# Last MLP in two phases, its first matrix as seven block products

## The chip, the cores and the metric

The kernel runs on one core of a Trainium2 chip. The core has five engines with a queue of instructions each: TensorE (PE, with its weight loads PEld shown apart), VectorE (DVE), ScalarE (ACT), GpSimd (POOL) and SyncE (SP), which issues nearly all DMAs here. The metric is device time in microseconds (us), the median of several runs.

## The reference

Two decoder layers on a sequence of 1024 tokens with 1024 features, all in float32. Each layer is a mixer (mLSTM in layer 0, latent attention in layer 1) and an MLP; the change is in the MLP of layer 1.

```python
def sqrelu_mlp(h, w1, w2):
    return jnp.square(jax.nn.relu(h @ w1)) @ w2
...
        h = modulate(rmsnorm(x, norm_g[l, 2]), sh2, sc2)
        y = sqrelu_mlp(h, mlp_w1[l], mlp_w2[l])
        x = x + g2[:, None, :] * rmsnorm(y, norm_g[l, 3])
```

`w1` is 1024 x 4096 and `w2` is 4096 x 1024.

## The kernel before

Tokens are worked on in two halves of 512. Activations lie with features on the partitions (eight blocks `k` of 128 features by 512 tokens); a tile `k4` or `hd` holds two such blocks. Every product is made of three passes (`mm3`, L230 to L233): each operand is split into a rounded high part (`hi`, type float32r) and a rest (`lo`), and the three matmuls `lo*hi`, `hi*lo`, `hi*hi` are summed in PSUM. ACT makes the high part by a cast (L189 for weights in `wsplit`, L470 in `split_mod`), DVE the rest by a subtraction (L190, L471).

Buffers are pools by tag: `k4` 24, `hd` 8, `ws` (split weights) 8, `raw` (loaded weights) 4, `tmc` 6, all in SBUF; in PSUM `ps` 2 and `pc` 2 of one bank, `pm` 2 of two banks. A tile that is asked for when all buffers of its tag are taken waits until one is released.

`mlp` (L941) yields steps. A *hidden* step makes one block of 128 hidden features by 512 tokens: one weight load of 512 KB and its split, 24 matmuls of 512 columns, relu, square and split. An *up* step takes finished hidden blocks times rows of `w2` into `y`. For the last half, groups of four are used: four hidden steps of a group are traced in turn with four up steps of the group before, and weights are loaded two steps ahead (`AHEAD`). With `rows=True` the result has tokens on the partitions.

A planner orders the instructions of each engine by a time model, by program order as priority; `tc.high_priority(PRIO)` moves instructions ahead by 300. PE's order is held by `go` (L1806): each step of a stream is issued behind the one before. `two_streams` (L1823) runs the other half's mixer between the steps of an MLP. Before the last MLP stands

```python
    two_streams(mlp(1, hfs[0], u0, [2] * 16, True), mixer1(hfs[1], z1, attention_second))
```

that is the first half's last MLP, with the second half's attention, output matrix, residual and norm (`post` L1751, `normed` L476) in it. Then comes the second half's MLP alone, with `all_out` as filler: at each step end one `next` of it. `x_to_rows` (L1564) loads each feature block of the residual stream, turns it by four PE transposes, copies it by ACT and stores it by token rows (`xr`); `rows_out` (L1593) reads those rows, forms the norm of a 128-token row block of the MLP's result (`u0` or `u1`), adds, and stores the output. The order is: turn of the first half, norm of the first half, turn of the second half, and behind the last matmul the norm of the second half.

Of the kernel before, what the change touches and what calls it, by code (L numbers as in the profile page):

```python
# [9 lines left out]
F32 = mybir.dt.float32  # L10
F32R = mybir.dt.float32r
# [3 lines left out]
ALU = mybir.AluOpType  # L15
# [67 lines left out]
def kernel(  # L83
# [54 lines left out]
    def tmc(dt=F32):  # L138
        return sb.tile([P, 512], dt, tag="tmc", bufs=TMC, name=f"tmc_{next(uid)}")
# [13 lines left out]
    def pm():  # L153
        return pp.tile([P, 2, 512], F32, tag="pm", bufs=2, name=f"pm_{next(uid)}")
# [72 lines left out]

    pe_last = [None]

    def mm3(o, lh, ll, rh, rl, start, stop):  # L230
        nc.tensor.matmul(o, ll, rh, start=start, stop=False)  # L231
        nc.tensor.matmul(o, lh, rl, start=False, stop=False)  # L232
        pe_last[0] = nc.tensor.matmul(o, lh, rh, start=False, stop=stop)  # L233


    nc.scalar.preload_act_table_set("natural_log_exp_and_others")
# [239 lines left out]
    def normed(h, xs_, rstd, A, sh):  # L476

        for k in range(KD):
            with paced():
                nc.vector.scalar_tensor_tensor(  # L480
                    xs_[k], xs_[k], A[:, k : k + 1], rstd, ALU.mult, ALU.mult
                )
                split_mod(h.hi[k], h.lo[k], xs_[k], sh[:, k : k + 1])
            if k % 4 == 3:
                yield 1

    def along_tokens(dst, y):
# [450 lines left out]
    NF = DFF // P  # L938
    AHEAD = 2

    def mlp(l, hf, y, sizes, rows=False):  # L941


        w1, w2, h = mlp_w1[l], mlp_w2[l], hf.h2
        hids = {}

        def hidden(f):
            def hid(w):
# [24 lines left out]
        def up_rows(fs, i, last):  # L973
# [40 lines left out]
            def out(ws):  # L1014
                for t in range(t0, t1):
                    if t % 2 == 0:
                        if t > t0:
                            yield "within"
                        b2 = pm()
                    block(b2[:, t % 2], ws, t)  # L1020
# [6 lines left out]
        def up_cols(fs, i, last):  # L1027
            G = len(fs)
            n = KD // G

            def out(w):
                for m in range(i * n, (i + 1) * n):
                    if m % 2 == 0:
                        if m > i * n:
                            yield "within"
                        b2 = pm()
                    pt = b2[:, m % 2]
# [8 lines left out]
        up = up_rows if rows else up_cols  # L1046
        steps, prev, f0 = [], [], 0
        for G in sizes:
            fs = list(range(f0, f0 + G))
# [8 lines left out]
        ready = []  # L1058
        for n in range(len(steps) + AHEAD):
            if n < len(steps):  # L1060
                ready.append(steps[n][0]())
            if n >= AHEAD:
                yield from steps[n - AHEAD][1](ready.pop(0))

                yield steps[(n - AHEAD + 1) % len(steps)][1].__name__


    rope_d = scratch([2, P, S], "rope_d")
# [494 lines left out]

    def x_to_rows(half):  # L1564

        for k in range(KD):
            a, b = tmc(), tmc()
            nc.sync.dma_start(a, xs_blk(k, half))
            yield
            pt = pc()  # L1570
            for t in range(4):
                nc.tensor.transpose(pt[:, ts(t, P)], a[:, ts(t, P)], ident)
            nc.scalar.copy(b, pt)
# [174 lines left out]
    A1 = gain(2, NG(0, 2), adac(0, SC2))  # L1748
    B1 = gate(3, NG(0, 3), adac(0, G2))

    def post(hf, y, B, src, A, sh):  # L1751
# [5 lines left out]
        yield 0  # L1757
        hf.h2 = Split()
        yield from normed(hf.h2, y, rstd, A, sh)

# [126 lines left out]
    rope_perm()  # L1887


    z1 = FH(claim=True)  # L1890
    ya = [None, None]

    def mixer1(hf, z, attention):
# [12 lines left out]
        for _ in wout(b_w_out[0], hf.o, lambda m, pt: evac(y[m], pt)):  # L1906
            yield 0
        yield 1
        yield from post(hf, y, B2, x_cols, A3, adac(1, SH2))
# [6 lines left out]
    u1 = FH(claim=True)  # L1916
# [46 lines left out]
```

## Time and profile before

| what | value |
|---|---|
| runs | 2396.41, 2397.75, 2398.75 us (median 2397.75) |
| profiled execution, first to last instruction | 2395.7 us |
| last MLP of the second half, first to last matmul | 2027.4 to 2387.2 us of the span |
| mean granted clock of PE | 0.997 |

The profiled execution has no time of its own beside its span; the three runs lie 0.7 to 3.1 us above the span. "Busy" is the time in which an engine works on at least one instruction; PE's matmuls overlap, so the distance between the starts of two is what one costs in a row. In a row of the groups view stand line, engine, operation, output<-inputs, shapes, count, then busy us and mean ns of one, then the engine's idle time just before and what ended it.

### The profile page before, as it was taken

The page shows a single profiled execution, that of the slowest core. Times are in us where ns is not written, and L with a number is a line of the kernel's source. Part 1 is how long each engine was busy: PE and PEld are TensorE (multiplying, and loading weights), DVE is VectorE, ACT ScalarE, POOL GpSimd, SP SyncE. Part 2 cuts the span into 40 slices and gives each one's busy share as a digit, 9 for nine tenths or more (in the row PEclk, how much of TensorE's full clock was granted, in tenths as well). Part 3 has the DMA queues.
Part 4 walks back from the last instruction along what each step waited for, and adds up shares of the span by engine and source line. Part 5 has one row for each costly group of instructions (what it writes and reads, how often), then busy time and mean ns, then how long its engine had stood idle before and what let it go on. Part 6 is the DMA issues. An engine that isn't in the chain of part 4 may idle for free.

```text
span 2395.7 us, 30518 instructions
## 1 busy us (share of the span) xinstructions
PE 2364.8 (99%) x11621; PEld 1945.5 (81%) x11621; DVE 1550.3 (65%) x2431; ACT 1054.9 (44%) x1712; POOL 18.3 (1%) x91
## 2 busy tenths in 40 slices
PE   7999999999999999999999999999999999999998
PEld 5888888788888887888888877888888888888886
DVE  6667866858656677877764867766566386353345
ACT  4355334655333454444444554344444353443333
POOL 1000000000000000000000000000000000000000
PEclk9999999999999999999999999999999999999999
DMA  8442654544654745545543444864424354354431
GB/s 310 148 143 81 192 178 134 165 132 150 189 171 152 243 138 179 159 160 186 168 137 114 153 162 153 260 240 133 139 97 150 105 167 128 101 189 140 144 99 62
DMA packets 377106, 374.48 MB, mean 156 GB/s; under 512 B 24355, under 2 KB 282464, under 8 KB 376960
## 3 DMA queue, kind: packets, MB, share of 16 engines
q1 hardware_dynamic: 376672, 372.44, 48.9%
q8 instruction: 91, 1.49, 0.3%
q14 instruction: 55, 0.45, 0.1%
q0 software_dynamic: 288, 0.10, 0.0%
HBM read 313.24 MB, written 59.24 MB: 155 GB/s over the span
## 4 chain that ended last, share of the span: by engine, by line
PE 91%; DVE 4%; DMA 3%; ACT 1%; issue 1%; SPq 0%; DVEq 0%; ACTq 0%
PE ps L231 17%; PE ps L232 17%; PE ps L233 17%; PE pm L231 10%; PE pm L232 10%; PE pm L233 10%; PE pc L1445 1%; PE pc L231 1%; PE pc L233 1%; PE pc L232 1%; PE pm L815 1%; PE pm L1331 1%; DMA raw<-in_mlp_w_dram 1%; DVE wl L190 1%; PE pm L1325 1%
## 5 line engine op out<-in xcount | busy, mean ns | idle before, releaser
L190 DVE TENSOR_TENSOR wl<-raw,wh 128x1024 fp32r<-128x1024 f32 (+2 forms) x366 | 438.7, 1202 | 449.5 <-ACT wh L189 442.3
L189 ACT CAST wh<-raw 128x1024 fp32r<-128x1024 f32 (+2 forms) x366 | 376.0, 1032 | 717.0 <-PE ps L231 392.2
L231 PE MATMUL ps<-k,wl 128*128 128x512 f32 x1528 | 611.0, 400 | 2.3 <-ACT k L671 1.4
L233 PE MATMUL ps<-k,wh 128*128 128x512 f32 x1528 | 601.0, 393 | 0.0
L232 PE MATMUL ps<-k,wh 128*128 128x512 f32 x1528 | 600.9, 393 | 0.0
L231 PEld LDWEIGHTS ps<-k,wl 128*128 128x128 f32 x1528 | 287.0, 188 | 69.7 <-issue 2.9
L233 PEld LDWEIGHTS ps<-k,wh 128*128 128x128 f32 x1528 | 287.0, 188 | 67.3 <-issue 0.5
L232 PEld LDWEIGHTS ps<-k,wh 128*128 128x128 f32 x1528 | 287.5, 188 | 63.6 <-issue 1.7
L198 DVE TENSOR_TENSOR k<-k,pm 128x512 f32<-128x512 f32 (+1 forms) x254 | 210.9, 859 | 107.0 <-PE pm L233 106.5
L231 PE MATMUL pm<-hd,wl 128*128 128x512 f32 x512 | 202.0, 394 | 0.4 <-ACT hd L470 0.4
L233 PE MATMUL pm<-hd,wh 128*128 128x512 f32 x512 | 199.8, 391 | 0.0
L232 PE MATMUL pm<-hd,wh 128*128 128x512 f32 x512 | 199.5, 390 | 0.2 <-DVE hd L471 0.2
L231 PE MATMUL pm<-wh,hd 128*128 128x512 f32 x488 | 192.9, 395 | 3.2 <-ACT raw L1337 2.9
L232 PE MATMUL pm<-wl,hd 128*128 128x512 f32 x488 | 191.3, 392 | 0.0
L233 PE MATMUL pm<-wh,hd 128*128 128x512 f32 x488 | 190.3, 390 | 0.0
L360 DVE SCALAR_TENSOR_TENSOR tma<-raw,cond,tma 128x512 f32<-128x512 f32 x168 | 125.6, 747 | 20.6 <-DMA raw<-in_kv_ada_w_dram 14.6
L471 DVE TENSOR_TENSOR hd<-tmp,hd 128x512 fp32r<-128x512 f32 x128 | 88.3, 690 | 56.8 <-ACT hd L470 56.5
L1337 ACT ACTIVATE raw<-pm,sm 128x128 f32<-128x128 f32 (+3 forms) x64 | 47.5, 742 | 151.3 <-DVE sm L1336 122.7
L232 PEld LDWEIGHTS pm<-hd,wh 128*128 128x128 f32 x512 | 96.2, 188 | 21.3 <-DVE hd L471 0.5
L231 PEld LDWEIGHTS pm<-hd,wl 128*128 128x128 f32 x512 | 96.1, 188 | 21.2 <-ACT hd L470 0.8
L233 PEld LDWEIGHTS pm<-hd,wh 128*128 128x128 f32 x512 | 96.1, 188 | 21.1
L231 PEld LDWEIGHTS pm<-wh,hd 128*128 128x128 f32 x488 | 91.6, 188 | 24.9 <-ACT raw L1337 5.5
(347 smaller groups left out, 3414.5 us busy)
## 6 DMA issues: line engine op xcount, KB each, us to landing
raw<-in_mlp_w_dram SPq DMA_DIRECT2D x256, 512.0 KB, 4.1
raw<-in_ada_w_dram SPq DMA_DIRECT2D x80, 512.0 KB, 4.3
raw<-in_a_w_in_dram SPq DMA_DIRECT2D x48, 512.0 KB, 4.1
xs<-k SPq DMA_DIRECT2D x40, 256.0 KB, 4.8
raw<-in_kv_ada_w_dram SPq DMA_DIRECT2D x16, 512.0 KB, 3.8
raw<-in_a_w_out_dram SPq DMA_DIRECT2D x16, 512.0 KB, 4.6
kd<-k SPq DMA_DIRECT2D x32, 256.0 KB, 3.7
vd<-k SPq DMA_DIRECT2D x32, 256.0 KB, 5.0
```

The costliest lines, as they stand in the source:

```text
L189: nc.scalar.copy(hi[:, :n], r[:, :n])
L190: i = nc.vector.tensor_sub(lo[:, :n], r[:, :n], hi[:, :n].bitcast(F32))
L198: return f(*a, **k)
L231: nc.tensor.matmul(o, ll, rh, start=start, stop=False)
L232: nc.tensor.matmul(o, lh, rl, start=False, stop=False)
L233: pe_last[0] = nc.tensor.matmul(o, lh, rh, start=False, stop=stop)
L360: nc.vector.scalar_tensor_tensor(acc, r[:, kk], cond[:, k : k + 1], acc, ALU.mult, ALU.add)
L471: nc.vector.tensor_sub(lo, u, hi.bitcast(F32))
L815: nc.tensor.matmul(nv[:, r, i], hf.PT[p_][:, r, cs], v[:, 2 * p_ + r], start=g == 0, stop=True,)
L1325: nc.tensor.matmul(o[:, :w], ql, kh, start=True, stop=False)
L1331: nc.tensor.matmul(o[:, :w], qh, kh, start=False, stop=True)
L1337: nc.scalar.activation(pr[:, :n], f, AF.Exp, bias=m, scale=SCALE, accum_out=l)
```

## The change

The second half's last MLP no longer alternates between its two matrices. It has two phases.

Phase one (`seven`) makes all 32 hidden blocks. For each pair of blocks, the product of `w1` (features in two halves, the two blocks) with the tokens' activations (features in two halves, tokens in two halves of 256) is seen as a 2 x 2 by 2 x 2 block product and made of seven block products (the form with few sums by Strassen and Winograd) instead of eight. Each product is four feature blocks of three passes, 12 matmuls of 256 columns. The weight sums are made from the two loaded blocks: two by GpSimd (`first`, because of `pool=True`), two by VectorE; then the two loaded blocks and the sums are split. Partial results are read from PSUM, and some products are summed on in the same PSUM bank (`more`). The products of a pair and of the pair before are issued in turn: 1 of the new, 5 of the old, 2, 4 of the old, 6, 3 of the old, 7. The finished hidden pair (maximum with zero, square) is stored to a DRAM scratch `hidd`.

The split weights of two of the sums, and of the second block's lower half, lie in `hd` buffers, beside the `ws` buffers.

The seven token blocks are made once by `quarters`, as the last part of the second half's mixer, in place of the norm's split: the normed values are kept in `y`, summed in place and split into 14 tiles of `k4`.

Phase two (`mlp` with `stored=True`) loads the hidden pairs again (`fetch`), splits them, and makes the up steps in groups of four.

The filler is arranged anew: both turns to rows run in phase one, one `next` at every third product, with the load of a block one ahead; the first half's norm and output run in phase two.

```diff
+    def split_wide(hi, lo, u):
+        nc.scalar.copy(hi, u)
+        nc.vector.tensor_sub(lo, u, hi.bitcast(F32))
...
+    def seven(l, pairs, B, out, pool=False):
...
+                r1, r2 = raw(), raw()
+                for r, f in ((r1, 2 * p_), (r2, 2 * p_ + 1)):
+                    nc.sync.dma_start(r.rearrange("p (a b) -> p a b", b=P), wcols(w1, f * P))
+                lo_, hi_ = slice(0, 512), slice(512, 1024)
+                A = wsplit(r1, 1024)
+                t1, t2 = raw(), raw()
+                first = nc.gpsimd if pool else nc.vector
+                first.tensor_add(t2[:, lo_], r2[:, lo_], r2[:, hi_])
+                first.tensor_sub(t1[:, lo_], r1[:, lo_], r2[:, lo_])
+                nc.vector.tensor_sub(t1[:, hi_], t2[:, lo_], r1[:, lo_])
+                nc.vector.tensor_sub(t2[:, hi_], r1[:, hi_], t1[:, hi_])
+                T1 = wsplit(t1, 1024)
+                if pool:
+                    a22, T2 = hd(F32R), (hd(F32R), hd(F32R))
+                    nc.scalar.copy(T2[0], t2)
+                    nc.vector.tensor_sub(T2[1], t2, T2[0].bitcast(F32))
...
+                nc.scalar.copy(a22[:, lo_], r2[:, hi_])
+                nc.vector.tensor_sub(a22[:, hi_], r2[:, hi_], a22[:, lo_].bitcast(F32))
...
+        def product(u, i):
+            o = {1: u.b, 6: u.b, 5: u.b, 3: u.b, 2: u.x, 7: u.z, 4: u.z}[i]
+            (wh, wl), (bh, bl) = u.w[i], B[i]
+            for k in range(4):
+                mm3(o, wh[:, k], wl[:, k], bh[k], bl[k], i in (1, 2, 7) and k == 0, k == 3, more=i not in (1, 2, 7))
+            with tc.high_priority(PRIO):
+                if i == 1:
+                    u.s1 = cut(tmc())
+                    nc.scalar.copy(u.s1, u.b)
+                elif i == 2:
+                    u.to = out(u.p_)
+                    nc.vector.tensor_add(u.to.c[0][0], u.s1, u.x)
+                elif i == 6:
+                    u.s16 = cut(tmc())
+                    nc.scalar.copy(u.s16, u.b)
+                elif i == 7:
+                    u.s7 = cut(tmc())
+                    nc.scalar.copy(u.s7, u.z)
+                elif i == 5:
+                    nc.vector.tensor_add(u.to.c[1][1], u.s7, u.b)
+                elif i == 4:
+                    nc.vector.tensor_add(u.to.c[1][0], u.s16, u.z)
+                else:
+                    nc.scalar.activation(u.to.c[0][1], u.b, AF.Relu)
+                    u.to.done()
...
+                cur.b = cut(ps())
+                m = pm()
+                cur.x, cur.z = cut(m[:, 0]), cut(m[:, 1])
+                if n + 1 < len(pairs):
+                    w = load(pairs[n + 1])
+            for u, i in ((cur, 1), (prev, 5), (cur, 2), (prev, 4), (cur, 6), (prev, 3), (cur, 7)):
+                if u:
+                    product(u, i)
+                    yield "hid"
+            prev = cur
...
+            def done():
+                nc.vector.tensor_scalar(s, s, 0.0, None, ALU.max)
+                nc.scalar.activation(s, s, AF.Square)
+                nc.sync.dma_start(hidd[hf.i, p_], s.rearrange("p a b -> p (a b)"))
...
+        def fetch(f):
+            with tc.high_priority(PRIO):
+                r, hi, lo = raw(), k4v(F32R), k4v(F32R)
+                nc.sync.dma_start(r, hidd[hf.i, f // 2])
+                split_wide(hi, lo, r.rearrange("p (a b) -> p a b", b=512))
...
     def all_out():
         yield from x_to_rows(0)
+        yield from x_to_rows(1)
         B3r = along_rows(B3)
-        yield
+        yield "rows"
         yield from rows_out(hfs[0], u0, B3r)
-        yield from x_to_rows(1)
         yield "last"
         yield from rows_out(hfs[1], u1, B3r)
...
-    dense = mlp(1, hfs[1], u1, [4] * 8, True)
+    dense, n = seven(1, range(NF // 2), blocks1, one_half(hfs[1]), True), 0
+    while go(dense) is not end:
+        n += 1
+        if n % 3 == 0 and v != "rows":
+            v = next(fill)
+    u1 = FH()
+    dense = mlp(1, hfs[1], u1, [], True, True)
+    next(dense)
     while (d := go(dense)) is not end:
         if v != "last" and d != "within":
             v = next(fill)
```

More of the change, by code (lines that the diff above doesn't have):

```diff
@@ L939, with ahead_of @@
     AHEAD = 2
-    def mlp(l, hf, y, sizes, rows=False):
+    hidd = scratch([2, NF // 2, P, 2 * H], "hidd")
+    def ahead_of(steps, primed=False):
+        ready = []
+        for n in range(len(steps) + AHEAD):
+            if primed and n == AHEAD:
+                yield "primed"
+            if n < len(steps):
+                ready.append(steps[n][0]())
+            if n >= AHEAD:
+                yield from steps[n - AHEAD][1](ready.pop(0))
+                yield steps[(n - AHEAD + 1) % len(steps)][1].__name__
@@ new lines, in both_halves, with done @@
+    def both_halves(p_):
+        o, s = Half(), [k4v(), hdv()]
+        o.c = [[s[0][:, 0], s[1][:, 0]], [s[0][:, 1], s[1][:, 1]]]
+        def done():
+            nc.vector.tensor_scalar(s[0], s[0], 0.0, None, ALU.max)
+            nc.vector.tensor_scalar(s[1][:, 1], s[1][:, 1], 0.0, None, ALU.max)
+            for i in range(2):
+                nc.scalar.activation(s[i], s[i], AF.Square)
+                nc.sync.dma_start(hidd[i, p_], s[i].rearrange("p a b -> p (a b)"))
+        o.done = done
+        return o
@@ L1057, in mlp @@
         steps += [up(prev, i, True) for i in range(len(prev))]
[L1058 to L1065, printed above, removed]
+        yield from ahead_of(steps)
     rope_d = scratch([2, P, S], "rope_d")
@@ L1757, in post @@
         yield 0
+        if kept:
+            yield from kept(y, rstd)
+            return
         hf.h2 = Split()
```

144 lines of the change are left out of this document (134 added, 10 removed).

## The prediction

> **What bounds the kernel now.** I read the page first: the span, the engines' shares and the chain that ended last.
>
> ```profile
> span 2395.7 us, 30518 instructions
> PE 2364.8 (99%) x11621; PEld 1945.5 (81%) x11621; DVE 1550.3 (65%) x2431; ACT 1054.9 (44%) x1712; POOL 18.3 (1%) x91
> PE 91%; DVE 4%; DMA 3%; ACT 1%; issue 1%; SPq 0%; DVEq 0%; ACTq 0%
> ```
>
> TensorE (PE) sets the end: 91% of the chain is PE, and GpSimd (POOL) is empty. The change touches the last stretch, so the next view is the busy time by windows; the columns are length, then busy time and count of each engine, granted clock, DMA share and GB/s.
>
> ```profile
> core 0: us, PE busy (x) PEld busy (x) DVE busy (x) ACT busy (x) POOL busy (x), PEclk, DMA share, GB/s
> 2027.40:2388.00 360.60, 359.77 (x1589) 293.43 (x1587) 155.44 (x222) 143.67 (x224) 0.00 (x0) 1.00 0.38 121
> 2388.00:2396.00 8.00, 0.00 (x0) 0.00 (x0) 3.99 (x10) 1.06 (x4) 0.00 (x0) 0.63 0.34 131
> ```
>
> The last MLP's second half is 360.6 us in which PE idles 0.8 us at full clock, while VectorE (DVE) and ScalarE (ACT) work 43% and 40% of it. The 8 us behind it are the last row block's norm and output; the change leaves their code alone. So what counts is how many matmuls stand there and how far apart they start. A matmul's duration (0.39 us) is no price, since the next starts before it ends; the timeline of PE gives starts. First and 48th matmul of the first matrix, then two of the second matrix, twelve steps apart:
>
> ```profile
> 2027.41 0.39 PE L231 MATMUL ps<-k,wl 128*128 128x512 f32 x1
> ...
> 2038.30 0.39 PE L233 MATMUL ps<-k,wh 128*128 128x512 f32 x1
> 2349.70 0.39 PE L232 MATMUL pm<-wl,hd 128*128 128x512 f32 x1
> ...
> 2352.42 0.39 PE L232 MATMUL pm<-wl,hd 128*128 128x512 f32 x1
> ```
>
> 10.89 / 47 = 0.2317 us each in the first matrix, 2.72 / 12 = 0.2267 in the second. Layer 0's value projection already issues 256-column matmuls with a new weight load each; these are 21 in a row, first and last:
>
> ```profile
> 300.97 0.28 PE L231 MATMUL ps<-wh,k 128*128 128x256 f32 x1
> ...
> 303.34 0.28 PE L233 MATMUL ps<-wh,k 128*128 128x256 f32 x1
> ```
>
> 2.37 / 20 = 0.1185 us, 51% of a 512-column one: halving the columns costs almost nothing in rate.
>
> **The change part by part.** *First matrix.* Before: 32 blocks of 24 matmuls, 768 x 0.2317 = 177.9 us. After: 16 pairs of seven products of 12 matmuls, 1344 x 0.1185 = 159.3 us, or 9.95 us a pair. That is **-18.6 us** as long as PE is fed. The second matrix keeps its 768 matmuls, and the 64 transposes of the row turn stay.
>
> *What a pair asks of the other engines.* The prices, DVE, then ACT, then POOL (mean ns behind the comma):
>
> ```profile
> L190 DVE TENSOR_TENSOR wl<-raw,wh 128x1024 fp32r<-128x1024 f32 x61 | 74.7, 1224 | 154.5 <-ACT wh L189 154.2
> L471 DVE TENSOR_TENSOR hd<-tmp,hd 128x512 fp32r<-128x512 f32 x32 | 22.1, 692 | 17.6 <-ACT hd L470 17.6
> L471 DVE TENSOR_TENSOR k<-ps,k 128x256 fp32r<-128x256 f32 x8 | 3.4, 421 | 0.9 <-ACT k L470 0.8
> L1339 DVE TENSOR_SCALAR raw<-raw,sm 128x1024 f32<-128x1024 f32 x8 | 6.0, 754 | 0.6
> L189 ACT CAST wh<-raw 128x1024 fp32r<-128x1024 f32 x61 | 64.0, 1049 | 173.5 <-PE ps L231 144.2 <-PE pm L232 27.7 <-DMA k<-xr 1.6
> L470 ACT CAST hd<-tmp 128x512 fp32r<-128x512 f32 x32 | 19.8, 620 | 1.0
> L663 ACT COPY k<-ps 128x256 f32<-128x256 f32 x16 | 6.0, 372 | 30.2 <-PE ps L233 30.1
> L508 ACT ACTIVATE pm<-k 128x1024 f32<-128x1024 f32 x4 | 4.1, 1028 | 3.0 <-DMA k<-in_x_dram 3.0
> L1573 ACT COPY tmc<-pc 128x512 f32<-128x512 f32 x12 | 7.0, 587 | 17.5 <-PE pc L1572 17.5
> L612 POOL MEMSET raw<- 128x1024 f32 x2 | 1.9, 954 | 146.9 <-DVE wl L190 146.9
> L1341 POOL MEMSET raw<- 128x128 f32 x32 | 6.6, 205 | 1087.8 <-DVE wl L190 483.8 <-DMA vd<-k 401.9 <-PE pc L1445 134.0
> ```
>
> DVE: three full splits (A, T1, T2) 3 x 1.224, the two sums left to it and the split of a22 3 x 0.692, three sums out of PSUM 3 x 0.421, the maximum 0.754: **7.77 us**, 78% of 9.95. ACT: three full casts 3 x 1.049, a22 0.620, three copies and the relu 4 x 0.372, the square 1.028, and the row turn's copy (16 blocks at one `next` per three products, 112 products: about 1.2 a pair) 0.69: **6.97 us**, 70%. POOL does two sums of 128x512; the trace has no two-input POOL instruction. From its memsets, (954 - 205) / 896 = 0.84 ns a written word; a sum passes two operands (lower bound, 2 x 512 x 0.84 + 98 = 0.95 us) or counts its write as well (three passes, 1.38). I take the middle, 1.17, so **2.34 us** a pair. No engine reaches PE's 9.95 by itself.
>
> *A rule against it.* In the Trainium skill, "SBUF — State Buffer", section "SBUF: two separate sides", a GpSimd instruction that reads SBUF and a DVE instruction with two SBUF inputs lock each other out for their whole length; and "GPSIMD Engine Reference", section "3.1 Elementwise — side-by-side cycle accounting", gives about 2.6 cycles an element, by which a sum would be about 1.2 us (an estimate). No run here shows either yet. Whether the engines take turns is decided in the second rival below, from rows.
>
> *Waits that are added.* Each pair keeps its ps bank through products 1, 6, 5 and 3, a product of the other unit's between each two, and three products (4.2 us) cover the reads of products 1, 6, 5 and 7. The last one has less: ps has two banks, and product 1 of the next-but-one pair takes the bank that the relu behind product 3 frees, with only product 7 (12 x 0.1185 = 1.42 us) between. The relu stands in ACT's queue among weight casts. Before, this happens and costs nothing; a hidden block's last matmul, the cast in front, the relu:
>
> ```profile
> 2032.74 0.39 PE L233 MATMUL ps<-k,wh 128*128 128x512 f32 x1
> 2032.71 1.05 ACT L189 CAST wh<-raw 128x1024 fp32r<-128x1024 f32 x1 [4.27 <-PE ps L231]
> 2033.66 0.60 ACT L957 ACTIVATE tmp<-ps 128x512 f32<-128x512 f32 x1
> ```
>
> The matmul ends at 2033.13 and the relu starts 0.53 us later, with a whole 5.6 us block as cover. In the new order, T2's cast waits for the very hd buffers that product 3 frees, so it tends to be ready together with the relu, and it was traced first. One cast in front: 0.28 (matmul) + 1.05 + 0.37 + about 0.04 for each of two hand-overs = 1.78 us after product 3's last start, against 0.12 + 1.42 = 1.54 of cover: 0.24 us of stall. None in front: 0. Two: 1.29. I take 0.3 a pair, x 16 = **+4.8 us** (0 to 20.6). A gain below zero has no source. Queued behind a late relu on ACT are the next casts, for which DVE's splits wait.
>
> The hand-over of 0.04 us is that of the last sum:
>
> ```profile
> 2386.78 0.39 PE L233 MATMUL pc<-wh,hd 128*128 128x512 f32 x1
> 2387.21 0.69 DVE L198 TENSOR_TENSOR k<-k,pc 128x512 f32<-128x512 f32 x1 [0.31 <-PE pc L233]
> ```
>
> *Preparing the seven token blocks.* The old norm's 8 subtractions go; 14 casts and 14 + 8 subtractions of 128x512 come: DVE 22 x 0.69 - 8 x 0.74 = +9.3 us, ACT +8.7 us. They run in the stage before, where the old norm's last row ends 45 us before the last MLP's first matmul (2027.41, above):
>
> ```profile
> 1981.63 0.74 DVE L474 SCALAR_TENSOR_TENSOR k<-k,ada,k 128x512 fp32r<-128x512 f32 x1
> ```
>
> So I cost this at 0; without that cover it would be 9 us, plus three more yields of two half steps.
>
> *Second phase.* A reload of hidden values is a 512 KB DMA, a 1.05 us cast and a 1.22 us subtraction; it replaces two 0.62 casts and two 0.69 subtractions of the old split. Per four blocks (96 x 0.2267 = 21.8 us): DVE 6 x 1.224 + 8 x 0.682 = 12.8 us, ACT 6.3. The first half's norm (four row blocks of about 3.6 us on DVE) enters over some six steps of 5.4 us, where DVE comes to 6.1 us a step; the excess of 4 us is taken up by the two pm pairs. 0, with 4 us if that cover fails.
>
> *Transfers.* All go through SyncE's queue: per pair two weight loads, one store of hidden values and 1.2 row-turn loads and stores, 2.1 MB in 9.95 us, 211 GB/s. The page's first slice moved 310, so the rate is there. Landing times:
>
> ```profile
> raw<-in_mlp_w_dram SPq DMA_DIRECT2D x256, 512.0 KB, 4.1
> k<-xr SPq DMA_DIRECT2D x8, 512.0 KB, 6.6
> ```
>
> The raw buffers are four, and one load uses all. From the second load's issue until T1's split frees a buffer: 4.1 + 2 x 1.17 + 0.69 + 1.05 + 1.22 + hand-overs 0.2 = 9.6 us, under 9.95 by little. This is the third rival.
>
> *Joints.* The first pair has four products instead of seven and its T1 is due 2.8 us in; the last three products follow each other without the other unit's between; hidden blocks for phase two need buffers that the token blocks give back. I take 1 us for each joint, **+2** (0 to 10).
>
> Sum: 2395.7 - 18.6 + 4.8 + 2 = 2383.9 us of span. The median of the runs, 2397.75, lies 2.05 above the profiled span; with that **2386 us**.
>
> **The rivals.** *First, the forecast:* PE paces phase one at 9.95 to 10.5 us a pair. For it: every engine's sum is below, and 256 columns ran at 0.1185 us. 0 stall gives 2395.7 - 18.6 + 2.05 = 2379; 0.6 us a pair and the joints give 2391. Chance 0.55.
>
> *Second, DVE and POOL take turns.* If every DVE instruction with two SBUF inputs keeps POOL out, the two cost 7.77 + 2.34 = 10.1 us a pair, and with some 6% idle in their waits on each other 10.7. The rule of the Trainium skill's "SBUF — State Buffer" (section "SBUF: two separate sides") would give this time. 16 x 10.7 = 171.2, so -6.7 + 2 + 2.05: 2393 (2386 at 10.1, and 2399 at 11.1). Against: the three sums from PSUM may lie beside POOL's. Chance 0.20.
>
> *Third, slower: the load loop through four raw buffers.* Its 9.6 us hold no foreign work, yet the same in-order DVE and ACT queues do 2.0 and 3.2 us of other work a pair; all of it in the loop gives 14.8, half 12.2. Half: 16 x 12.2 = 195.2 less one load's head start of some 5 us is 12 us above 177.9: 2412. It decides from 177.9 / 16 = 11.1 us a pair. Against: the loop's members are traced ahead with priority, and a22's split, which holds the second buffer longest, can go early. Chance 0.17.
>
> *Fourth, the gain is taken and given back at the joint* to phase two: reloads wait for token blocks' buffers, a landing (4.1) plus cast and subtraction (2.3), twice over: 2386 + 7 = 2393. Against: 24 k4 buffers hold 14 + 4 + 1 there, five free. Chance 0.08.
>
> **How the numbers follow.** About 0.2%, 4.8 us, is what a measurement tells from no change: below 2393.0 is faster, above 2402.5 slower. Faster: 0.55, half of the second (0.10) and 0.03 of the fourth, 0.68. Slower: the third, less a little, 0.16. Same: the rest, 0.16. The range goes from 2377 (a little under no stall) to 2402: it leaves out most of the third rival and some 0.03 below. The likeliest case alone: 2379 to 2391.
>
> **What would show it.** Right: in the window of phase one, matmuls 0.118 us apart, about 160 to 168 us for 1344 of them, gaps of 0.2 to 0.5 us in front of the first product's matmul with the relu as releaser. Second rival: DVE rows longer than 1.22 and 0.69 while POOL works, DVE over 90% busy, PE waiting for DVE's splits. Third: ACT and POOL waiting for weight DMAs whose issue waited for DVE. Fourth: one gap of PE over 3 us at the start of the row products. Wrong altogether: starts of 256-column matmuls over 0.13 us apart, or norm work of the token blocks still running when phase one should begin.

## The result, and the profile after

The change makes the kernel **slower**: 2419.16 us (median of 4 runs, 2417.95 to 2420.95) against 2397.4 us, a ratio of 1.0085 with a 95% interval of 1.0071 to 1.0099. The forecast was 2386, and the range ended at 2402. Of e1's four runs below, one took 3314 us at a granted clock of 0.65; e1 is given by the median of the other three, 2414.45 us, where texts put on record before later runs have 2415.8, with that run counted in.

The page of the changed kernel: span, busy time and share of each engine, then the shares of the chain that ended last.

```profile
span 2417.7 us, 32187 instructions
...
PE 2361.1 (98%) x12197; PEld 1966.6 (81%) x12197; DVE 1676.1 (69%) x2573; ACT 1098.1 (45%) x1774; POOL 65.0 (3%) x119
...
PE 78%; DMA 9%; DVE 8%; issue 3%; ACT 2%; POOL 0%; SPq 0%; DVEq 0%; ACTq 0%; POOLq 0%
```

TensorE's share of the chain fell from 91 to 78%, though over the whole span it is busy about as long as before. DMA, VectorE and ScalarE stand in the chain in its place. The windows view, cut at the first and last matmul of phase one and at the end of the second matrix, says where:

```profile
core 0: us, PE busy (x) PEld busy (x) DVE busy (x) ACT busy (x) POOL busy (x), PEclk, DMA share, GB/s
2030.74:2230.30 199.56, 178.83 (x1413) 172.75 (x1412) 149.94 (x178) 107.62 (x173) 41.53 (x28) 0.97 0.60 188
2230.30:2409.00 178.70, 178.70 (x770) 144.18 (x768) 117.07 (x166) 71.00 (x99) 0.00 (x0) 1.00 0.58 197
```

Before, both matrices and the row turn took 359.8 us (2027.4 to 2387.2). The terms of the prediction make 171.9 us for phase one: 159.3 of products, 4.8 of stall, and the transposes of the row turn, 7.8 us (359.8 less 177.9 less 768 x 0.2267). It took 199.6: **27.7 us too many, 1.7 us a pair**. TensorE is idle for 20.7 us, where the sum had 4.8 of stall, and busy for 178.8, where the sum had 167.1. Part of the longer busy time is the clock: behind three of the gaps the granted clock is lower for about 3 us, and 256-column matmuls start 0.21 us apart there (columns as above, the clock third from the end):

```profile
2049.60:2052.80 3.20, 3.20 (x16) 3.20 (x17) 3.20 (x3) 1.23 (x2) 2.40 (x2) 0.54 0.00 0
2147.71:2151.38 3.67, 3.67 (x19) 3.67 (x19) 3.67 (x3) 1.32 (x2) 2.99 (x2) 0.56 0.24 76
2223.16:2226.07 2.91, 2.91 (x16) 2.91 (x15) 2.46 (x5) 2.91 (x5) 0.00 (x0) 0.51 0.69 246
```

Some 40 matmuls at 0.21 instead of 0.1185 us make about 4 us; the rest of the longer busy time was not taken apart. The lower clock stands only behind gaps, and e6's phase one, nearly without them, runs at 1.00; that the gaps bring it was not tested by itself.

Phase two should have taken 174.1 and took 178.7, without one idle microsecond: **4.6 too many**. Phase one starts 3.3 us later than before, where 2 were allowed for joints, and the tail is 0.2 longer: 33.8 us, the whole miss of the span. Of the 3.3 us, 2.8 stand already at the 9000th matmul, in stages that the change leaves alone; in the profiled executions of all the kernels here that matmul starts between 1803.5 and 1809.8 us. So the joint itself cost 0.5.

Who makes TensorE wait in phase one: the view of waits (what waited, for whom; us in total, times, longest).

```profile
...
ACT hd L1083 <- DVE hd L1082: 32.5, 13, 4.0
ACT wh L189 <- DMA raw<-in_mlp_w_dram: 29.3, 15, 3.2
DVE wl L190 <- ACT wh L189: 24.6, 26, 3.5
PEld pm L232 <- DVE hd L1042: 21.4, 16, 3.5
PE pm L232 <- DVE hd L1042: 17.5, 13, 3.2
...
ACT hd L1017 <- DMA hidd<-hd: 6.7, 9, 2.2
```

In nearly every pair, product 7, the first that writes the second bank of the pair's pm tile, waits for L1042, VectorE's sum of product 2 out of the first bank. That product ended three products earlier; its sum is late because it stands in VectorE's queue behind L190, the split of A, which waits for the cast L189, which waits for the weights to land. A round in the timeline: a pair's two weight loads, and all that follows until the next pair's second load (start, duration, engine, line, operation, tiles; in brackets the idle time before it and who ended it; rows between are left out):

```profile
2103.39 0.38 SPq L1005 DMA_DIRECT2D raw<-in_mlp_w_dram  x1
...
2105.01 0.42 SPq L1005 DMA_DIRECT2D raw<-in_mlp_w_dram  x1
...
2107.97 1.05 ACT L189 CAST wh<-raw 128x1024 fp32r<-128x1024 f32 x1 [2.15 <-DMA raw<-in_mlp_w_dram]
2109.05 1.23 DVE L190 TENSOR_TENSOR wl<-raw,wh 128x1024 fp32r<-128x1024 f32 x1 [1.35 <-ACT wh L189]
...
2110.20 0.41 DVE L1042 TENSOR_TENSOR hd<-tmc,pm 128x256 f32<-128x256 f32 x1
2110.37 1.28 POOL L1010 TENSOR_TENSOR raw<-raw 128x512 f32<-128x512 f32 x1 [8.32 <-DVE wl L190]
2110.53 1.67 DVE L1023 TENSOR_TENSOR hd<-raw,hd 128x512 fp32r<-128x512 f32 x1
...
2110.66 0.39 PE L232 MATMUL pm<-k,wl 128*128 128x256 f32 x1 [1.32 <-DVE hd L1042]
...
2112.33 1.63 POOL L1011 TENSOR_TENSOR raw<-raw,raw 128x512 f32<-128x512 f32 x1 [0.68 <-POOL raw L1010]
2112.72 1.78 DVE L1012 TENSOR_TENSOR raw<-raw,raw 128x512 f32<-128x512 f32 x1
...
2114.59 1.05 ACT L189 CAST wh<-raw 128x1024 fp32r<-128x1024 f32 x1 [0.44 <-DVE raw L1012]
...
2115.68 1.23 DVE L190 TENSOR_TENSOR wl<-raw,wh 128x1024 fp32r<-128x1024 f32 x1 [0.45 <-ACT wh L189]
...
2116.93 0.41 SPq L1005 DMA_DIRECT2D raw<-in_mlp_w_dram  x1
```

This is the loop of the third rival, and it takes 11.92 us from second load to second load, not 9.6. It is 5.36 us until GpSimd starts on what the load brings (4.1 in the sum); from there to the end of L1012 it is 4.13 us (3.03 in the sum, 2 x 1.17 + 0.69); cast, split and hand-overs are 2.43, as priced. The profile's own chain goes round by the first load instead, in the same 11.9 us (2103.39 to 2115.30): its landing (4.5), A's cast, product 2's sum L1042 behind A's split, the split of the previous pair's a22 (L1023), L1012, L1013, and with r1 free the next first load. Both ways share the raw buffers and VectorE's queue, and the change runs at the pace of both. Beside GpSimd, VectorE's own instructions are stretched as well; the groups view of phase one (busy time, mean ns of one, then idle time before and its releaser):

```profile
L1012 DVE TENSOR_TENSOR raw<-raw,raw 128x512 f32<-128x512 f32 x14 | 24.9, 1777 | 5.4 <-POOL raw L1010 5.4
L1011 POOL TENSOR_TENSOR raw<-raw,raw 128x512 f32<-128x512 f32 x14 | 22.6, 1612 | 2.7 <-POOL raw L1010 2.7
L1010 POOL TENSOR_TENSOR raw<-raw 128x512 f32<-128x512 f32 x14 | 19.3, 1382 | 129.0 <-DMA raw<-in_mlp_w_dram 76.5 <-DVE hd L1042 16.9 <-DVE wl L190 16.7
L1082 DVE TENSOR_SCALAR hd<-hd 128x1024 f32<-128x1024 f32 x15 | 18.0, 1197 | 0.1
```

L1012 is a sum that costs 0.69 us elsewhere and takes 1.78 here; the one-input maximum L1082 (0.75) has a mean of 1.20.

### The profile page after: what moved, and what is told of

Same layout as the page of the kernel before. It is cut to its first block, busy times and chain, and to the rows that moved or that the text cites. A ratio compares the mean times of both kernels' runs of the same rounds, so it can differ in the third digit from the quotient of the medians.

```text
span 2417.7 us, 32187 instructions
## 1 busy us (share of the span) xinstructions
PE 2361.1 (98%) x12197; PEld 1966.6 (81%) x12197; DVE 1676.1 (69%) x2573; ACT 1098.1 (45%) x1774; POOL 65.0 (3%) x119
## 4 chain that ended last, share of the span: by engine, by line
PE 78%; DMA 9%; DVE 8%; issue 3%; ACT 2%; POOL 0%; SPq 0%; DVEq 0%; ACTq 0%; POOLq 0%
PE ps L232 14%; PE ps L233 13%; PE ps L234 13%; PE pm L232 9%; PE pm L233 9%; PE pm L234 9%; DMA raw<-in_mlp_w_dram 6%; DVE wl L190 1%; ACT wh L189 1%; PE pc L1677 1%; DVE tma L361 1%; DVE raw L1012 1%; PE pc L232 1%; PE pc L234 1%; PE pc L233 1%
## 5 line engine op out<-in xcount | busy, mean ns | idle before, releaser
L190 DVE TENSOR_TENSOR wl<-raw,wh 128x1024 fp32r<-128x1024 f32 (+2 forms) x366 | 438.3, 1201 | 342.0 <-ACT wh L189 335.6
L189 ACT CAST wh<-raw 128x1024 fp32r<-128x1024 f32 (+2 forms) x366 | 375.8, 1032 | 622.5 <-PE ps L232 246.3
L232 PE MATMUL ps<-k,wl 128*128 128x512 f32 (+1 forms) x1400 | 546.1, 390 | 2.3 <-ACT k L690 1.4
L234 PE MATMUL ps<-k,wh 128*128 128x512 f32 (+1 forms) x1400 | 536.9, 383 | 0.0
L233 PE MATMUL ps<-k,wh 128*128 128x512 f32 (+1 forms) x1400 | 536.6, 383 | 0.0
L232 PEld LDWEIGHTS ps<-k,wl 128*128 128x128 f32 x1400 | 263.5, 188 | 59.6 <-issue 3.1
L234 PEld LDWEIGHTS ps<-k,wh 128*128 128x128 f32 x1400 | 263.4, 188 | 56.0 <-issue 0.5
L233 PEld LDWEIGHTS ps<-k,wh 128*128 128x128 f32 x1400 | 263.9, 189 | 53.2 <-issue 1.9
L198 DVE TENSOR_TENSOR k<-k,pm 128x512 f32<-128x512 f32 (+1 forms) x254 | 210.5, 857 | 74.4 <-PE pm L234 73.8
L232 PE MATMUL pm<-wh,hd 128*128 128x512 f32 x256 | 102.1, 399 | 4.3 <-ACT raw L1569 2.2
L234 PE MATMUL pm<-wh,hd 128*128 128x512 f32 x256 | 100.0, 391 | 0.0
L233 PE MATMUL pm<-wl,hd 128*128 128x512 f32 x256 | 99.8, 390 | 0.0
L1169 ACT ACTIVATE tmp<-ps 128x512 f32<-128x512 f32 x96 | 56.9, 593 | 79.8 <-PE ps L234 79.6
L472 DVE TENSOR_TENSOR hd<-tmp,hd 128x512 fp32r<-128x512 f32 x96 | 66.7, 695 | 36.0 <-ACT hd L471 35.7
```

Source lines behind the costliest of these rows:

```text
L189: nc.scalar.copy(hi[:, :n], r[:, :n])
L190: i = nc.vector.tensor_sub(lo[:, :n], r[:, :n], hi[:, :n].bitcast(F32))
L198: return f(*a, **k)
L232: nc.tensor.matmul(o, ll, rh, start=start, stop=False, **m)
L233: nc.tensor.matmul(o, lh, rl, start=False, stop=False, **m)
L472: nc.vector.tensor_sub(lo, u, hi.bitcast(F32))
```

## The experiments

Three causes could stretch the pair. **Loop**: the four raw buffers are a ring (load, sums, cast, split, load), as above. **Lock**: GpSimd and VectorE keep each other out. **Bank**: one pm tile for two banks. A fourth came up in the first runs, the **hidden round**: T2's cast needs an hd tile, and those are held by hidden pairs until their store to DRAM has landed. Each kernel was timed against before on its own chip; the ratio has its 95% interval.

### Sums, engine and bank, one at a time

e1 gives T1 and T2 tiles of the k4 pool, e2 gives GpSimd's two sums to VectorE, e3 does both, e4 gives product 2 a bank of its own (pc).

```diff
-                t1, t2 = raw(), raw()
+                t1, t2 = k4()[:, :1024], k4()[:, :1024]        # e1, e3
-                first = nc.gpsimd if pool else nc.vector
+                first = nc.vector                               # e2, e3
-                m = pm()
-                cur.x, cur.z = cut(m[:, 0]), cut(m[:, 1])
+                cur.x, cur.z = cut(pc()), cut(pm()[:, 0])       # e4
```

> The two weight sums t1 and t2 lie in k4 buffers, so the four raw buffers hold loaded weights alone. Loop theory (a load's buffers are given back only at the end of a queue of DVE work that stands behind the next load's own split, 12.2 us round): the round opens, a pair costs PE's 9.95 us plus transposes and small stalls, 10.4 to 10.9; phase one falls from 199.6 us to 167 to 175 and the time to 2387 to 2395 us. Lock theory (DVE and GpSimd taking turns is the limit by itself): the sums stay on GpSimd, DVE needs 7.8 us and GpSimd's 3.0 us stand beside it, 10.8 and more a pair with waits, 2405 us or more.

> GpSimd's two sums go to VectorE, buffers as in the changed kernel. Loop theory: the round keeps its members, loses the lock-outs (split of a22 0.92 to 0.69, maximum 1.20 to 0.75, first sum 1.78 to 0.69) and gains two sums of 0.69: about 0.4 to 1.0 us a pair less, 2402 to 2413 us. Lock theory: all of it goes, a pair costs 10.0 to 10.8, 2385 to 2395 us.

> Both: sums in k4 buffers and made by VectorE. Loop theory: as with the k4 buffers alone within 5 us, 2385 to 2395 us, since DVE's sum of 9.2 us a pair is still under PE's 9.95. Lock theory: as with the sums on VectorE alone.

> Products 2 and 7 of a pair write two PSUM tiles (pc and pm) instead of the halves of one, so that product 7 no longer waits for the reading of product 2's sum, the wait in which the trace shows PE idle. Loop theory: that wait is only where the round's lateness shows; PE then waits for the split weights instead, 2414 to 2421 us. Bank theory (the shared tile is the cause): 1.5 us a pair go, 2393 to 2398 us.

Measured: e1 2414.45 us (1.0072, 1.0055 to 1.0089), e2 2420.96 (1.0096, 1.0081 to 1.0111), e3 2404.44 (1.0027, 1.0017 to 1.0037), e4 2410.67 (1.0056, 1.0040 to 1.0072). In time, neither the loop alone nor the lock alone is worth much: 5 us and nothing; together they win 15, so something else stops each. e1 lies within the lock theory's bounds, e2 and e3 above those of both theories, and e4 between its two.

The time hides part of e1. Its phase one, from its first matmul to phase two's first, takes 190.2 us, 9.3 less than the change's (e2 202.9, e3 187.8, e4 191.9), but it begins later: from the 9000th matmul to phase one e1 takes 229.4 us, the change 223.6. So keeping T1 and T2 out of the raw buffers did shorten phase one, and e11 below shows where the 5.8 us go.

In e4 the wait for L1042 is gone, and what I had priced comes out in its place, the bank that the relu gives back late (waits of e4):

```profile
PE ps L232 <- ACT hd L1054: 8.4, 9, 1.5
```

The chain of waits of e3 shows the third stop (start, duration, what):

```profile
2150.29 1.07 ACT hd L1083
...
2151.38 5.15 DMA hidd<-hd
...
2156.60 1.06 ACT hd L1017
```

The square L1083 of a hidden pair, its store to DRAM (5.15 us), and only then T2's cast L1017, which waited for that hd tile. In the change the casts L1017 wait 6.7 us for such stores, in nine pairs (above); in e1, with the raw round open, 29.7 us in thirteen. The prediction knew that T2's cast waits for hd tiles; it overlooked that a DMA lies in between.

### The hidden pairs out of hd

e5 is the change with hidden pairs in k4 tiles, and nothing else; e6 is e5 with e1's and e2's edits; e7 is e6 with e4's; e11 is e6 with GpSimd's sums back.

```diff
-            o, s = Half(), hdv()
+            o, s = Half(), k4v()
```

> Of the changed kernel only the finished hidden pairs move, from hd to k4 buffers, so that the split weights in hd no longer wait for a store to DRAM. Loop theory in its first form (the raw buffers' round alone sets the pair): that round is untouched, 2416 to 2421 us. Two-round theory (the hd buffers' round, square, store, cast of T2, is as long and the two hold each other up in the same queues): it still stands behind the raw round, 2412 to 2420 us; a fall under 2410 would say that the hd round was the first.

> Weight sums in k4 buffers and made by VectorE (2404 us so far), and now the hidden pairs in k4 as well. Two-round theory: the second round opens, what is left is product 7's wait for the shared PSUM tile, 10.5 to 10.9 us a pair, 2393 to 2399 us. If the hd round were only a symptom: 2402 to 2406 us as without it.

> As the one before, and products 2 and 7 in PSUM tiles of their own. Two-round theory: no round is left under 10.4 us a pair but the relu's late hand-back of ps, 10.3 to 10.8, phase one 166 to 172 us, 2386 to 2394 us: below the kernel before. If the queues of DVE and ACT are full by themselves (9.2 and 7.0 us of work a pair): 2398 us or more.

> As the kernel with all buffers open (2387.0), but the two first sums of a pair are GpSimd's again, as in the change. Buffer theory: with both rounds open the lock-out of GpSimd and VectorE delays nothing that is due, VectorE is at 7.8 plus some 2 to 3 us of blocked time of 9.95, and the time is 2386 to 2392. Engine theory (my second rival, the two engines take turns, 10.1 to 11.1 us a pair): 2393 to 2402.

Measured: e5 2406.27 us (1.0034, 1.0021 to 1.0048), e6 **2386.96** (0.9955, 0.9940 to 0.9970), e7 2387.45 (0.9953, 0.9938 to 0.9967), e11 2391.27 (0.9969, 0.9956 to 0.9982). With both rounds open the change is faster than before. By the text on record for e5, a time under 2410 says that the hidden round was the first; but e5's phase one takes 187.8 us, as e3's does, so the two rounds are about equally long, 11.7 us a pair. e6 came out 6 us below what was expected, since product 7's wait went too. Windows of e6, phase one and phase two:

```profile
2028.09:2198.40 170.31, 168.83 (x1414) 167.67 (x1413) 134.89 (x201) 107.54 (x170) 0.00 (x0) 1.00 0.66 207
2198.40:2376.12 177.72, 177.72 (x769) 143.84 (x767) 119.24 (x169) 72.00 (x103) 0.00 (x0) 1.00 0.61 205
```

Phase one is 170.3 us, where the prediction's terms gave 171.9. The banks are worth 8 us on the change and nothing on e6: product 7's wait for the shared tile costs time only where the weights are late. With both rounds open the lock costs phase one nothing: e11, with GpSimd's sums, takes as long there. What it loses to e6, 4.3 us, lies ahead of phase one. Its window, and the gap of TensorE in the last up step of the stage before, in e11 and then in e6:

```profile
2033.11:2203.29 170.18, 168.98 (x1414) 167.60 (x1413) 125.85 (x172) 106.29 (x169) 35.21 (x26) 1.00 0.65 203
```

```profile
2018.48 0.77 PE L232 MATMUL pm<-wh,hd 128*128 128x512 f32 x1 [3.73 <-DVE k L198]
```

```profile
2015.93 0.47 PE L232 MATMUL pm<-wh,hd 128*128 128x512 f32 x1 [1.11 <-DVE k L198]
```

The first pairs' weight sums run there ahead of L198, the sums that free pm for the old stage, and beside GpSimd they hold VectorE longer. Behind that gap the granted clock is lower as well: 0.89 in the last 30 us ahead of phase one, 1.00 in e6. From the 9000th matmul to phase one e11 takes 228.8 us and e6 223.8; e1 and e3, which differ in the same way, take 229.4 and 223.7. The change does not lose this (223.6), as its sums wait for raw buffers.

### The phases alone

e8 keeps the phases but multiplies the first matrix by 512 columns as before, with the old norm and split, and one `next` of the filler at every second step. e13 is e8, and e10 is e6, with the reloaded hidden values of phase two in hd tiles.

```diff
-    dense, n = seven(1, range(NF // 2), blocks1, one_half(hfs[1]), True), 0
+    dense, n = up_front(1, hfs[1], range(NF // 2)), 0           # e8, e13
...
-                r, hi, lo = raw(), k4v(F32R), k4v(F32R)
+                r, hi, lo = raw(), hdv(F32R), hdv(F32R)         # e10, e13
```

> The two phases, the reload of hidden values and the moved filler without block products: phase one makes the hidden blocks by 24 matmuls of 512 columns as before, with the old norm and split. Every theory here: the phases cost little, 2396 to 2404 us; more than 2406 would move the loss from the block products to the phases.

> As the phases alone (first matrix by 512-column matmuls, 2403.0), but with the reloaded hidden values in hd tiles. If the operand's tile is what the phases alone cost: 768 x 0.005 = 3.8 us less, 2398 to 2400, which is the time of before. If the cost is the norm or the reloads themselves: 2402 to 2404.

> As the kernel with all buffers open (2387.0), but the hidden values that phase two reloads are split into hd tiles instead of k4 tiles. In the traces so far the second matrix's matmuls start 0.232 us apart where the hidden operand lies in a k4 tile and 0.227 us apart where it lies in an hd tile (before). If the tile decides: 0.227 again, 768 x 0.005 = 3.8 us less, 2382 to 2384. If something else in phase two does (the reloads' transfers, the norm beside it): 0.232 stays and 2386 to 2388. If eight hd buffers are too few for the reloads: gaps of TensorE in phase two and over 2388.

Measured: e8 2402.96 us (1.0014, 1.0005 to 1.0024), e13 2397.87 (1.0001, 0.9992 to 1.0011), e10 2386.33 (0.9948, 0.9933 to 0.9963). The phases by themselves cost some 3 to 4 us (e8), and the tile of the hidden operand is what costs it (e13). Here that operand is the one loaded into TensorE, 128 columns of it at a time; the 512 columns that move past it are `w2`'s, and lie in a `ws` tile in both. Two matmuls of the second matrix, twelve steps apart, in the change and then in e10:

```profile
2330.20 0.39 PE L232 MATMUL pm<-wh,k 128*128 128x512 f32 x1
...
2333.00 0.39 PE L232 MATMUL pm<-wh,k 128*128 128x512 f32 x1
```

```profile
2329.65 0.39 PE L232 MATMUL pm<-wh,hd 128*128 128x512 f32 x1
...
2332.37 0.39 PE L232 MATMUL pm<-wh,hd 128*128 128x512 f32 x1
```

2.80 / 12 = 0.2333 us against 2.72 / 12 = 0.2267, which is the step of before. Over the whole phase it is 178.7 / 768 = 0.2327 in the change, 177.7 / 768 = 0.2314 in e6 and 174.1 / 768 = 0.2267 in e10. In e10's windows phase two is 3.6 us shorter than e6's:

```profile
2202.64:2376.73 174.09, 174.09 (x768) 143.80 (x767) 117.99 (x167) 68.76 (x99) 0.00 (x0) 1.00 0.60 205
```

Its median is only 0.6 us below e6's, and the two are not told apart by time; in these profiled executions e10 enters phase one 3.3 us later than e6, all of it from the early stages named above. So the step is shown by the windows and by e13 against e8, not by e10's time.

### What the raw round is made of

e12 is e6 with T1 and T2 back in raw buffers (VectorE sums, hidden pairs in k4). It should have come near e6, and did not; so e14 to e19 took the round apart. e14 is e12, e15 the change and e16 e5, each with the second weight load issued ahead of the first; e17 is e14 with e10's edit. e18 is e12 without the store of hidden pairs: phase two loads as many bytes of `w1` in their place, so what it multiplies is not phase one's result. e19 is e12 with T1 alone in a k4 tile.

```diff
-                for r, f in ((r1, 2 * p_), (r2, 2 * p_ + 1)):
+                for r, f in ((r2, 2 * p_ + 1), (r1, 2 * p_)):               # e14 to e17
-                nc.sync.dma_start(hidd[hf.i, p_], s.rearrange("p a b -> p (a b)"))   # e18
...
-                nc.sync.dma_start(r, hidd[hf.i, f // 2])                     # e18
+                nc.sync.dma_start(r.rearrange("p (a b) -> p a b", b=P), wcols(w1, f * P))
...
-                t1, t2 = raw(), raw()
+                t1, t2 = k4()[:, :1024], raw()                              # e19
```

> As the kernel with all buffers open (2387.0), but T1 and T2 come from the four raw buffers again (sums by VectorE, hidden pairs in k4). With GpSimd's sums and raw buffers (hidden pairs in k4) it was 2406, a raw round of 11.5 us. Without GpSimd's two steps (1.29 and the blocked 1.77 give way to sums of 0.69) the round comes to about 10.2 to 10.8 us: loop theory 2389 to 2397. If the raw round is no limit once the hidden pairs are out of hd and GpSimd is out of the way: 2386 to 2388.

> As the kernel with VectorE's sums, hidden pairs in k4 and the four raw buffers (2407.3), but each pair's second raw load is issued ahead of its first. In that kernel's trace SyncE issues the first load when the last sum L1013 ends (2106.96), then the store of hidden values (its square ends at 2108.12), and only then the second load (2108.58), whose buffer was free from the end of L1011 (2105.16); it lands 6.3 us later and all four sums wait for it: 10.9 to 11.2 us a round. Queue-order theory: the second load goes out some 3 us earlier, the round falls to 8 to 9 us, TensorE paces, 2387 to 2391. Landing theory (two loads and a store share the transfers, 6 to 7 us whatever the order): 2403 to 2409.

> The change with only the order of the two loads swapped. In the change the second load is issued 1.6 us behind the first and lands 5.3 us later; GpSimd's two sums and the blocked VectorE sum follow, 11.9 us a round. Queue-order theory: this opens the raw round as two k4 tiles for T1 and T2 did (2415.8), but the round of the hidden pairs through hd holds on: 2413 to 2418. If the raw round was the only one: 2387 to 2395. Landing theory: no change, 2417 to 2421.

> The change with the order of the loads swapped and the hidden pairs in k4 tiles, GpSimd's sums and the four raw buffers kept. Queue-order theory: both rounds are open, as in the kernel that had k4 tiles for both and kept GpSimd (2391.3): 2390 to 2396. Landing theory: as with hidden pairs in k4 alone (2406.3): 2403 to 2408.

> The swapped order, VectorE's sums, hidden pairs in k4, and the reloaded hidden values of phase two in hd tiles (matmul steps of 0.227 instead of 0.232 us, 3.8 us less there). Queue-order theory: 2383 to 2387, the best of all kernels here; landing theory: 2399 to 2405.

> As the kernel with VectorE's sums, hidden pairs in k4 and four raw buffers (2407.3), without the store of the hidden pairs to DRAM; phase two loads the same bytes from the weights instead, so the hidden values it uses are not those of phase one. In that kernel a pair's second raw load is issued when T1's split frees its buffer, lands 6.2 to 7.7 us later (the first takes 4.0 to 4.8), and the sums, the cast and the split of T1 (2.1 + 1.05 + 1.3) and 0.4 us behind the store on SyncE close a round of 11 us. Landing theory (the store goes out between the two loads and shares the transfers): the second load lands in about 5 us, the round is some 9.5 to 9.9 us, 2388 to 2396. If the store has no part in it: 2404 to 2409.

> As the same kernel (2407.3), with T1 alone in a k4 tile and T2 in a raw buffer. Ring theory: three of the four raw buffers are taken by a pair, so the second load no longer waits for T1's split but for the last sum or less, and the first goes out a pair ahead; the round falls by the cast and split of T1 (2.3 us) and more, below TensorE's 10.4: 2386 to 2391. If the round is something else (the store, T2, the queues): 2398 to 2409.

Measured: e12 2407.25 us (1.0036, 1.0025 to 1.0047), e14 2409.98 (1.0054, 1.0037 to 1.0070), e15 2416.47 (1.0077, 1.0060 to 1.0094), e16 2424.23 (1.0105, 1.0090 to 1.0120), e17 2407.91 (1.0037, 1.0024 to 1.0050), e18 2403.86 (1.0021, 1.0012 to 1.0031), e19 **2390.80** (0.9962, 0.9947 to 0.9977).

The queue-order theory (the second load goes out too late because of its place in SyncE's queue) fell with e14, e16 and e17. They also lie above the bounds of the landing theory, e16 by 16 us: with GpSimd's sums kept, the swapped order costs 18 us (e5 2406.3), and why so much was not followed up. The second load does not wait for its own old buffer, as I had read it; it takes the one that T1's split frees, and swapped, the load that A and all but one of the sums need waits for it instead. e15 is the one number inside the bounds of that theory, but its interval overlaps the change's own, so it bears nothing out.

The landing is part of the round. Landing of the weight loads in the same 169 us (median, last number) before, in the change, in e12 and in e18:

```profile
raw<-in_mlp_w_dram SPq DMA_DIRECT2D x29, 512.0 KB, 4.0
```

```profile
raw<-in_mlp_w_dram SPq DMA_DIRECT2D x27, 512.0 KB, 5.1
```

```profile
raw<-in_mlp_w_dram SPq DMA_DIRECT2D x28, 512.0 KB, 5.4
```

```profile
raw<-in_mlp_w_dram SPq DMA_DIRECT2D x32, 512.0 KB, 4.8
```

A pair's two loads go out within 1.6 us of each other, with a store between or beside them, where before had no such store and moved 121 GB/s in its last stage; phase one moves 188. Without the store the loads land 0.6 us sooner, but the time falls by 3 us, not by 11 to 19. The chain of waits of e18 shows what fills the round then:

```profile
2091.62 5.09 DMA raw<-in_mlp_w_dram
...
2096.80 0.06 DVE raw L1010
...
2097.41 1.22 DVE wl L190
2098.63 0.33 DVE k L1052
2098.96 0.61 DVE hd L1023
...
2099.60 0.69 DVE raw L1011
2100.29 0.60 DVE raw L1012
...
2101.41 0.69 DVE raw L1013
2102.10 1.20 DVE wl L190
...
2103.32 5.16 DMA raw<-in_mlp_w_dram
```

From issue to issue it is 11.7 us, against 11.9 in the change. Between L1010 and L1011, both of the round, VectorE's queue does A's split, a sum out of PSUM and the split of a22, 2.2 us of work that is not the round's, and L1013 stands ahead of T1's split. This is foreign work of the kind that the third rival named, though only the sum out of PSUM is among the work that it counted. Neither GpSimd's sums (e5 to e12: no gain) nor the store nor the order is *the* term; the queues fill what one leaves. The link is the buffer: with T1 elsewhere, a pair needs three raw buffers of four, and the time is 2390.8.

## Why the prediction was wrong

**The step that failed** is the one on transfers: "9.6 us, under 9.95 by little", and with it the forecast that TensorE paces phase one. The round measured 11.92 us. Of the 2.3 us missing, 1.3 lie between the load's issue and the first sum (4.1 was the median of the whole span, and beside this phase's own transfers a load takes longer), 1.1 in the three sums, where GpSimd and VectorE stretch each other. The sum of a loop that held 96% of the bound, made of medians and of no work in between, was no evidence for "under". Beside it stands a term at nothing: the prediction has T2's cast wait for the hd buffers that product 3 frees, and leaves out that they come free only when the hidden pair's store has landed, 5.15 us in e3's chain. That is a second round of about the same length. A third loss that the sum did not have stands behind the waits: some 4 us at a lower granted clock, with starts over the 0.13 us that the prediction names as a sign of being wrong.

**The rival that came nearest** is the third. Its sign is there: ACT and GpSimd wait for weight loads, and the first load's issue waits for VectorE's L1013. Its price, 2412 for half of the foreign work against 2419 measured, is near by luck: its 2.0 us of VectorE's foreign work are the sums out of PSUM and the maximum, while A's and a22's splits, which stand in the rounds above, are neither in its loop nor in that figure, and the 2.3 us that the loop lacked in the change are landing and stretch. Nor does "traced ahead with priority" take A's split out of the queue. It was also not alone. The hidden round through hd was not in the list, and opening only one of the two rounds gives 2404.4 (e3) and 2406 to 2407 (e5, e12); both, 2387.0.

**The second rival**, turns of VectorE and GpSimd, has its mechanism in the rows and not its price, and VectorE is 75% busy in phase one, not over 90%. The Trainium skill, "SBUF — State Buffer", section "SBUF: two separate sides", has the two engines lock each other out; this trace agrees: 1.78 us for L1012 instead of 0.69. But e11 takes 170.2 us for phase one with it: a lock-out costs where VectorE is waited for, and here that is 4 to 5 us ahead of phase one, a lower clock there counted in. **The fourth**, a gap at the start of the row products, did not come: phase two has no idle time of TensorE.

**Second phase at nothing**: "the second matrix keeps its 768 matmuls" held for the count, and not for the step. The hidden operand moved from hd to k4 tiles, and 0.2267 us became 0.2327 in the mean; the prediction's own rows had shown 0.2317 for a k4 operand, there the moving one. The reloads and the norm cost nothing, as forecast.

**GpSimd's sum**, 1.17 us between 0.95 and 1.38: the mean in the change is 1.38 and 1.61; 0.3 us a sum too low, and for L1011 above the upper bound.

**The stall at the relu**, 0.3 us a pair: in the change another wait comes ahead of it; in e4 it is 8.4 us in all, against 4.8 forecast, and in e6 TensorE's idle time is 1.5 us in the whole phase. **The reads said to be covered by three products**, those of products 1, 6, 5 and 7, leave out product 2's: product 7 shares its tile and waits for that read, which three products in between did not cover once VectorE was late.

**Right**: the rate of 256-column matmuls (168.8 us busy in e6, against 159.3 + 7.8), the preparation of the token blocks under cover (no token-block work holds the first product), and the joint (0.5 us, between 0 and 10; 2 taken). With both rounds open the kernel takes 2387.0 where 2386 was forecast; but part of that is luck, as phase two's 3.6 us are set off by a stall and a joint smaller than priced.

**Two sums** are off, and change nothing: the second rival at 10.1 us a pair gives 2383, not 2386, and the transfers of a pair are 2.2 MB, 221 GB/s, not 2.1 and 211 (phase one moved 188 in the change, 207 in e6).

## What to carry to other kernels

A ring of buffers is a loop with its own time: add up one turn of it with the landing under the load that the change itself makes and with what in-order queues put between its members, and call it safe only if that is well below the engine that should set the pace. When one stop is removed and nothing happens, look for a second loop of the same length: here two edits of 5 and 13 us alone were worth 28 together (e1 2414.5, e5 2406.3, e11 2391.3 against 2419.2). Read it in the stage itself, too: e1's 9 us in phase one showed as 5 in the time. A tile of several banks, or a tile that a DMA must empty, makes its next user wait for the slowest of its readers.

## What the runs showed of the hardware

In phase two a 512-column matmul starts 0.2314 us (e6) to 0.2327 us (the change) after the one before in the mean if the hidden values that it loads lie in a k4 tile, and 0.2267 if they lie in an hd tile (e10). k4 tiles are 1040 words a row and hd tiles 1024; whether their place or their length makes the difference was not tried.

In phase one of the change a GpSimd sum of 128x512 takes 1.28 us at the shortest and 1.75 at the longest; VectorE's own sum beside it goes from 0.69 to 1.78, and a maximum with one input from 0.68 to 1.78 at worst. Behind three waits of TensorE the granted clock was 0.51 to 0.56 for about 3 us, and 256-column matmuls started 0.21 us apart instead of 0.12; behind other waits of 1.1 to 1.8 us it stayed at 1.00. A 512 KB load lands after 5.1 us in the median of phase one and after 4.0 in the same stretch of before.
